# A hybrid encoder trunk on one core: the front re-cut into steps of two chunks, low parts on VectorE, kept parts in long rows

## The chip, the cores and the metric

The kernel runs on one core of one Trainium2 chip. The time is that of one execution on the device, in microseconds (us); lower is better. The engines are PE (TensorE: matrix products, with PEld as its weight loads), DVE (VectorE), ACT (ScalarE), POOL (GpSimd) and SP (SyncE, which here issues most transfers). Each engine takes its instructions strictly in program order and waits at the first one whose inputs are not there. Before the change: 1161.26 us, the median of 3 runs (1159.34 to 1162.54).

## The reference, cut to what matters

Two sequences of 512 rows (prompt and sample, 1024 wide) go through one layer with the same weights.

```
mod = silu(c) @ w_ada + b_ada                       # 1024 -> 6*1024
sh1, sc1, g1, sh2, sc2, g2 = split(mod, 6)
h = rms_norm(x, norm1_g) * (1 + sc1) + sh1
proj = h @ w_in                                     # 1024 -> 2816 columns
q_a, k_a, v_a, q_r, k_r, v_r, g_r = split(proj)     # the first 768 columns: q_a (512), k_a, v_a (128 each)
o_a = windowed_attention(q_a, k_a, v_a, sink)       # distance bias, |t-s| <= 128
o_r = bidirectional_retention(q_r, k_r, v_r, g_r, decay_fwd, decay_bwd)
x = x + g1 * (concat(o_a, o_r) @ w_out)
x = x + g2 * (relu(rms_norm(x, norm2_g)*(1+sc2)+sh2 @ w_mlp1)^2 @ w_mlp2)
y = rms_norm(x, final_g)
```

Products run in near fp32 precision: each fp32 operand is split into a high part (a cast) and a low part (operand minus high part), and a product is three matmuls, high by high, low by high and high by low.

## The kernel before, in words

The 1024-wide contraction is cut into eight chunks of 128, kc = 0 to 7. What this text calls the front runs from the start to the end of the first 768 projected columns of the prompt. It has to do three things that hang on one another, chunk by chunk.

*Modulation sums.* Only the shift and scale columns of w_ada are needed first. For chunks 0 and 1 there is one sum each (`one`); from chunk 2 on a pair of chunks has a scale sum (`pair(kc, 1)`, tiles named ..._1) and a shift sum (`pair(kc, 0)`, tiles ..._0). A pair's sum, in `ada_sums` (L206 to L239), is a generator in three steps: 16 small matmuls into `pm` (L216; 8 with high weights `wh_ada`, 8 with low weights `wl_ada`, the first 8 on one half of the rows, kh = 0, the last 8 on the other, kh = 1) and a copy by ACT of the sum to `mr` (L221); two transposes by PE into `pmt` (L229); and four small DVE operations that leave the shift or scale columns `mod_s`, `mod_a` (L232, L234, L202, L204). A weight tile's high part is a cast by ACT (`high_pair`, L97); its low part (`low_pair`, L1001) is a subtraction by DVE for kh = 0 and by POOL for kh = 1.

*Modulated chunks.* `prepare(kc)` calls `modulated` (L323): DVE forms `hm` = x transposed times scale plus shift (L326), ACT casts the high part `h` (L327), DVE subtracts for the low part (L328).

*Products.* `products(kc, c0, c1)` multiplies chunk kc by columns c0 to c1 of six column groups (L128 to L130, three matmuls each, into six open accumulators `first`). Its weights come from `split_wi(kc)`: the high part `wih` by DVE (ACT for chunk 0), the low part `wil` by POOL for all but one chunk. After the sixth column group, ACT issues two transfers that keep the previous chunk's `wih` and `wil` in `kept_first` (L1047), so that the sample sequence can read them back (`kept_unit`, L119) instead of splitting them again. There `kept_first` is laid out by column group: a partition's write is six pieces of 512 B, a partition's read one row of 4 KB.

Two side tasks run in between: the table of distance biases (`masked_distance` on DVE, L503, and eight ACT operations `bias_t`, L514, taken one at a time by `next(tables)`) and the retention decays (`log_decays`, L521).

The order on each engine is the order in which the code is written: everything from `start` to `pin(start)` is left as it stands, and a scheduler places only later work. So what stands ahead of what is set by the loop at L1104 to L1183.

Of the kernel before, what the change touches and what calls it, by code (L numbers as in the profile page):

```python
# [15 lines left out]
P = 128  # L16
# [14 lines left out]
def trunk_kernel(ctx, tc, x0, x1, c0, c1, w_ada, b_ada, norm1_g, w_in, attn_sink, decay_f, decay_b,  # L31
# [38 lines left out]
    def f(ap):  # L70
        return ap.bitcast(F32)
# [82 lines left out]
    dec = const.tile([P, 2, RH], F32, name="dec")  # L154
    nc.gpsimd.dma_start(dec[:, 0, :], decay_f.broadcast_to([P, RH]))
    nc.gpsimd.dma_start(dec[:, 1, :], decay_b.broadcast_to([P, RH]))
    sink = const.tile([P, AH], F32, name="sink")
    nc.gpsimd.dma_start(sink, attn_sink.broadcast_to([P, AH]))

# [343 lines left out]
    def masked_distance():  # L503
        nc.vector.tensor_scalar(sink8, sink, 8.0, None, ALU.mult)
# [132 lines left out]
    def proj_unit(hT, col, name, done):  # L637
        key = f"in{col}"

        def load():  # L640
            if hT is hT_of[1]:
                return kept_unit(key, name, P)
            return split_unit(cols_unit(w_in, 0, KC, col, P), name, nc.vector)
# [44 lines left out]
    def ret_v_units(hT, b):  # L688
# [3 lines left out]
        def unit(kq):  # L692
            key = f"rv{kq}"

            def load():
                if b == 1:
                    return kept_unit(key, f"rv{b}_{kq}", 512)
                return split_unit(cols_unit(w_in, kq * 2, 2, 1792, 512), f"rv{b}_{kq}", nc.vector)

# [36 lines left out]
    def out_units(b, late=None):  # L736
# [10 lines left out]
        def unit(hf, kq):  # L747
# [224 lines left out]

    xt0 += [load_x_tile(0, t) for t in range(2, NT)]
    wi, pairs = {}, {}
# [31 lines left out]

    def low_one(kc, kh, engine):
        t, w = ones[kc][kh]
        engine.tensor_sub(w[1], t, f(w[0]))
        ones[kc][kh] = [x.rearrange("p (c k n) -> p c k n", c=2, n=P) for x in w]  # L1010
# [6 lines left out]

    def split_wi(kc, engine=nc.vector, low=nc.gpsimd):
        w = [r4(f"wi{s}_{kc}").rearrange("p a n -> p (a n)")[:, :768] for s in "hl"]
        if engine is nc.scalar:  # L1020
            nc.scalar.copy(w[0], wi[kc][:, :768])
        else:
            nc.vector.tensor_copy(w[0], wi[kc][:, :768])
        low.tensor_sub(w[1], wi[kc][:, :768], f(w[0]))
        wi[kc] = w

    def take_xT(kc, pt):
        if kc % 2 == 0:
            pair = r4(f"xT_{kc}", F32)
            xT.extend([pair[:, 0, :], pair[:, 1, :]])  # L1030
        if kc % 2 == 0:
            nc.scalar.copy(xT[kc], pt)
        else:
            nc.vector.tensor_copy(xT[kc], pt)
# [4 lines left out]
    def products(kc, c0, c1):  # L1039
# [29 lines left out]
    cond = conditioning()  # L1069
    r0 = x_rstd(0, 0, xt0[0])  # L1070
    r1 = x_rstd(0, 1, xt0[1])
    x_scale(xt0[0], r0)
    next(cond)
    x_columns(0)
    next(cond)
    x_scale(xt0[1], r1)
    x_columns(1)
    r2 = x_rstd(0, 2, xt0[2])
    next(cond)
    r3 = x_rstd(0, 3, xt0[3])  # L1080
    x_scale(xt0[2], r2)
# [8 lines left out]
    split_wi(0, nc.scalar)  # L1090
    low_one(0, 1, nc.vector)
    for kc in range(4):
        take_xT(kc, banks[kc])
# [12 lines left out]
    first = attn_units(hT[0], 0)
# [3 lines left out]
    next(one1)  # L1110
    products(0, 1, 2)
# [8 lines left out]
    split_wi(2)  # L1120
    load_pair(4)
    load_wi(4)
    load_wi(5)
    g = pair(2, 1)
    next(g)
    products(1, 0, 1)
    next(g)
    high_pair(4, 1)
    g = pair(2, 0)
    next(g)  # L1130
    products(1, 1, 2)
    next(g)
    next(tables)
    prepare(2)
    low_pair(4, 1, 0, nc.vector)
    low_pair(4, 1, 1, nc.gpsimd)
    split_wi(3)
    prepare(3)
    products(1, 2, 6)
    logs = log_decays()  # L1140
    for kc in range(4, KC, 2):
        high_pair(kc, 0)
        low_pair(kc, 0, 0, nc.vector)
        if kc > 4:
            next(logs)
        low_pair(kc, 0, 1, nc.gpsimd)
        products(kc - 2, 0, 3)
        g = pair(kc, 1)
        next(g)
        products(kc - 2, 3, 5)  # L1150
        next(g)
        next(tables)
        split_wi(kc)
        if kc > 4:
            next(logs)
        products(kc - 2, 5, 6)
        g = pair(kc, 0)
        next(g)
        if kc + 2 < KC:
# [8 lines left out]
        next(logs)
        if kc + 2 < KC:
            low_pair(kc + 2, 1, 0, nc.vector)  # L1170
            low_pair(kc + 2, 1, 1, nc.gpsimd)
        split_wi(kc + 1, low=nc.gpsimd if kc == 4 else nc.vector)
        next(logs)
        prepare(kc + 1)
        next(logs)
        next(tables)
        products(kc - 1, 1, 6)
    next(tables)
    pin(start)
# [298 lines left out]
```

## Time and profile before

| | before |
|---|---|
| median of 3 runs | 1161.26 us |
| the profiled execution: its time, and its span | 1161.89 us, 1160.1 us |
| PE busy in the span | 1109.4 us (96%) |
| DVE, ACT, POOL busy | 933.4, 494.0, 69.0 us |
| PE's first matmul, first product, end of the front | 10.43, 23.27, 82.32 us |
| PE's granted clock, mean | 0.992 |

A share of busy time is an average; it is the idle time of PE, and what ended each piece of it, that tells what a stage waits for. In a row such as `65.20 0.28 PE L229 ... [2.13 <-ACT mr L221]` the first number is when the instruction starts, the second how long it takes, and the bracket how long the engine sat idle just before it and whose result ended that. "PEclk" is the clock granted to TensorE: 1.00 is the higher of its two levels (2.4 GHz), 0.50 the lower (1.2 GHz). POOL's 13 long operations of the front (six `wl_ada`, seven `wil`) all lie before 71 us.

### The profile page before, as it was taken

The numbers are of one execution on the slowest core, as the hardware profiler recorded it, in microseconds if no ns is written. First come the engines' busy times: TensorE is split into PE (matmuls) and PEld (weight loads), VectorE is DVE, ScalarE is ACT, GpSimd is POOL, SyncE is SP. The second block draws the span as 40 slices with busy tenths as digits, with TensorE's granted clock in tenths as the row PEclk, the third lists the DMA queues.
The fourth block names the chain that finished last, engine by engine and source line by source line (L and its number), as shares of the span: only waits on it lengthen the run. The fifth ranks groups of instructions, "written<-read, shape, count | busy, mean of one in ns | idle before, by whom it ended". The sixth has DMA issues, their size and how long they took to land.

```text
span 1160.1 us, 14470 instructions
## 1 busy us (share of the span) xinstructions
PE 1109.4 (96%) x5167; PEld 903.8 (78%) x5167; DVE 933.4 (80%) x1550; ACT 494.0 (43%) x846; POOL 69.0 (6%) x79
## 2 busy tenths in 40 slices
PE   5899999999999999999999999999999999999975
PEld 3578787777888788888788888888778888888854
DVE  5888988978888697689998778866696866968896
ACT  4456765435563234346333333332455333432341
POOL 3620001000000000000000000000000000000012
PEclk9999999999999999999999999999999999999988
DMA  9796677655455489941654455443866364464413
GB/s 289 238 283 211 214 230 272 218 193 190 155 167 199 156 303 333 343 148 46 214 204 155 164 165 189 155 163 103 287 230 237 106 195 137 144 200 139 184 37 145
DMA packets 124112, 224.37 MB, mean 193 GB/s; under 512 B 8500, under 2 KB 59780, under 8 KB 124040
## 3 DMA queue, kind: packets, MB, share of 16 engines
q1 hardware_dynamic: 111144, 217.14, 55.8%
q10 hardware_dynamic: 12544, 6.29, 1.9%
q8 instruction: 40, 0.66, 0.3%
q0 software_dynamic: 352, 0.03, 0.1%
q14 instruction: 32, 0.26, 0.1%
HBM read 152.36 MB, written 71.06 MB: 193 GB/s over the span
## 4 chain that ended last, share of the span: by engine, by line
PE 75%; DVE 11%; DMA 5%; issue 3%; ACT 3%; POOL 2%; SPq 0%; ACTq 0%; DVEq 0%; POOLq 0%
PE px_None L936 12%; PE x L1310 12%; PE py_None L936 9%; PE y L1310 9%; PE po L129 2%; PE po L130 2%; PE po L128 2%; DMA raw_ada_g<-in_w_ada_dram 2%; PE po L429 1%; PE ppt L422 1%; PE psc L396 1%; PE pj_rq L129 1%; PE pj_rq L128 1%; PE pj_rv L128 1%; PE pj_rv L130 1%
## 5 line engine op out<-in xcount | busy, mean ns | idle before, releaser
L841 ACT CAST uc_0h<-ur 128x1024 fp32r<-128x1024 f32 x28 | 29.4, 1050 | 67.9 <-PE x L1310 38.1
L1310 PE MATMUL x<-wc_0l,uc_0h 128*128 128x512 f32 x128 | 50.7, 396 | 5.4 <-DVE wc_0l L842 5.4
L1310 PE MATMUL x<-wc_0h,uc_0h 128*128 128x512 f32 x128 | 50.5, 396 | 3.9 <-DVE acc L1356 3.2
L128 PE MATMUL po<-wh_wo,ms 128*128 128x512 f32 x128 | 50.5, 397 | 1.9 <-ACT ms L761 1.9
L1310 PE MATMUL x<-wc_1h,uc_1h 128*128 128x512 f32 x128 | 50.3, 394 | 1.0 <-ACT wc_1h L841 1.0
L1310 PE MATMUL x<-wc_1l,uc_1h 128*128 128x512 f32 x128 | 50.2, 392 | 0.5 <-DVE wc_1l L842 0.5
L1310 PE MATMUL x<-wc_0h,uc_0l 128*128 128x512 f32 x128 | 50.3, 393 | 0.0
L1310 PE MATMUL x<-wc_1h,uc_1l 128*128 128x512 f32 x128 | 50.1, 391 | 0.0
L129 PE MATMUL po<-wl_wo,ms 128*128 128x512 f32 x128 | 49.8, 391 | 0.3 <-DVE wl_wo L103 0.3
L842 DVE TENSOR_TENSOR uc_0l<-ur,uc_0h 128x1024 fp32r<-128x1024 f32 x28 | 34.2, 1222 | 19.6 <-ACT uc_0h L841 15.9
L130 PE MATMUL po<-wh_wo,ms 128*128 128x512 f32 x128 | 49.6, 390 | 0.0
L255 DVE SCALAR_TENSOR_TENSOR adacc_c<-raw_ada_c,cact,adacc_c 128x512 f32<-128x512 f32 x56 | 39.8, 748 | 6.7 <-DMA raw_ada_c<-in_w_ada_dram 5.7
L841 ACT CAST wc_s4h<-raw_w 128x1024 fp32r<-128x1024 f32 x16 | 16.8, 1053 | 62.8 <-PE px_None L936 46.1
L406 ACT ACTIVATE st<-st,negm 128x256 f32<-128x256 f32 (+1 forms) x64 | 35.2, 556 | 18.8 <-DVE negm L401 18.8
L841 ACT CAST wc_0h<-w 128x1024 fp32r<-128x1024 f32 x24 | 25.2, 1049 | 42.4 <-DVE w L1289 16.3
L255 DVE SCALAR_TENSOR_TENSOR adacc_g<-raw_ada_g,cact,adacc_g 128x512 f32<-128x512 f32 x56 | 40.3, 747 | 2.1 <-DMA raw_ada_g<-in_w_ada_dram 1.8
L842 DVE TENSOR_TENSOR wc_0l<-w,wc_0h 128x1024 fp32r<-128x1024 f32 x24 | 29.3, 1221 | 13.5 <-ACT wc_0h L841 13.4
L936 PE MATMUL py_None<-hch,wc_a 128*128 128x512 f32 x120 | 39.7, 390 | 0.1
L936 PE MATMUL px_None<-hch,wc_a 128*128 128x512 f32 x120 | 39.6, 391 | 0.0
L936 PE MATMUL px_None<-hch,wc_s 128*128 128x512 f32 x120 | 39.4, 389 | 0.0
L1310 PE MATMUL y<-wc_1l,uc_1h 128*128 128x512 f32 x96 | 37.5, 391 | 0.6 <-DVE wc_1l L842 0.6
L1310 PE MATMUL y<-wc_0h,uc_0h 128*128 128x512 f32 x96 | 37.6, 392 | 0.0
(397 smaller groups left out, 3484.8 us busy)
## 6 DMA issues: line engine op xcount, KB each, us to landing
ur<-spill SPq DMA_DIRECT2D x56, 512.0 KB, 4.3
raw_w<-in_w_mlp_dram SPq DMA_DIRECT2D x32, 512.0 KB, 3.8
spill<-s SPq DMA_DIRECT2D x64, 256.0 KB, 3.7
w<-in_w_mlp_dram SPq DMA_DIRECT2D x32, 512.0 KB, 5.4
spill<-u SPq DMA_DIRECT2D x48, 256.0 KB, 2.3
raw_ada_g<-in_w_ada_dram SPq DMA_DIRECT2D x16, 512.0 KB, 4.3
raw_ada_c<-in_w_ada_dram SPq DMA_DIRECT2D x16, 512.0 KB, 4.0
raw_ada<-in_w_ada_dram SPq DMA_DIRECT2D x12, 512.0 KB, 8.8
```

Source lines behind the costliest of these rows:

```text
L128: nc.tensor.matmul(ps, lhs[0], rhs[0], start=start, stop=False)
L129: nc.tensor.matmul(ps, lhs[0], rhs[1], start=False, stop=False)
L130: nc.tensor.matmul(ps, lhs[1], rhs[0], start=False, stop=stop)
L255: nc.vector.scalar_tensor_tensor(acc[b], src, cb, acc[b], ALU.mult, ALU.add)
L396: nc.tensor.matmul(psc[:, :w], qs[hh][:, isl], k_[:, s, j0 * P:j1 * P], start=(s == 0), stop=(s == 1))
L406: nc.scalar.activation(st[hh][:, :w], st[hh][:, :w], AF.Exp, bias=negm[:, hh:hh + 1], scale=0.125, accum_out=den[:, hh:hh + 1])
L422: nc.tensor.transpose(pt[:, hh * P:(hh + 1) * P], st[hh][:, jj * P:(jj + 1) * P], ident)
L429: nc.tensor.matmul(po, va[:, j0 + jj, g].rearrange("p s e -> p (s e)"), pts[jj][:, s, :], start=(jj == 0 and s == 0), stop=(jj == nj - 1 a ...
L841: nc.scalar.copy(hi, src)
L842: nc.vector.tensor_sub(lo, src, f(hi))
L936: self.last = nc.tensor.matmul(bank[:, cs], x[:, k, :], y, start=first and k == 0 and i == 0, stop=last and k == 3 and i == 2, skip_group_ ...
L1310: nc.tensor.matmul(out, u[x][:, i % 2, ts_], w[y][:, i % 2, :], start=first and i == 0 and k == 0, stop=end and i == GP - 1 and k == 2, sk ...
```

## The change

The diff, without its renamed arguments and with the start of the front cut:

```
-                nc.scalar.dma_start(kept_first[:, :, s, k*P:(k+1)*P], f(wi[k][s]).rearrange(...))
-    kept_first = tc.dram_tile((P, 6, 2, 1024), F32, name="kept_first")
+                nc.scalar.dma_start(kept_first[:, s, k, :], f(wi[k][s]))
+    kept_first = tc.dram_tile((P, 2, KC, 768), F32, name="kept_first")

 def modulated(which, b, kc, src):
+    if which == b == kc == 0:                # chunk 0: two ACT activations straight from xT
+        for d in (dst[:, 0, :], t):
+            nc.scalar.activation(d, src, AF.Identity, bias=mod_s..., scale=mod_a...)
+        nc.vector.tensor_sub(dst[:, 1, :], t, f(dst[:, 0, :]))
+        return dst

-def low_pair(kc, s, kh, engine):             # low_one likewise
-    engine.tensor_sub(w[1], t, f(w[0]))
+def low_pair(kc, s, kh):
+    nc.vector.tensor_sub(w[1], t, f(w[0]))

-def split_wi(kc, engine=nc.vector, low=nc.gpsimd):    # high part: DVE (ACT for chunk 0), low: POOL
+def split_wi(kc):
+    nc.scalar.copy(w[0], wi[kc][:, :768])
+    nc.vector.tensor_sub(w[1], wi[kc][:, :768], f(w[0]))

     prepare(1)
+    low_pair(2, 1, 1)
     high_pair(2, 0)
-    low_pair(2, 0, 0, nc.vector)
-    low_pair(2, 0, 1, nc.gpsimd)
-    products(0, 2, 6)                        # and the hand-written steps for chunks 1 to 3, and the old loop
...
+    low_pair(2, 0, 0)
+    low_pair(2, 0, 1)
+    head_loads()                             # decays and sinks, on POOL's queue; before, at the start
+    tables, logs = None, log_decays()
+    for kc in range(2, KC, 2):
+        sums_a, sums_b = pair(kc, 1), pair(kc, 0)
+        more = kc + 2 < KC
+        next(sums_a)
+        products(kc - 2, 3 if kc == 2 else 0, 4 if kc == 2 else 3)
+        if more:                             # the loads of the next pair and its two chunks
+            load_pair(kc + 2); load_wi(kc + 2); load_wi(kc + 3)
+        next(sums_a)
+        split_wi(kc)
+        next(sums_b)
+        products(kc - 2, 4 if kc == 2 else 3, 6)
+        split_wi(kc + 1)
+        if more:
+            high_pair(kc + 2, 1); low_pair(kc + 2, 1, 0)
+        if kc > 2:
+            next(logs); next(logs)
+        next(sums_b)
+        prepare(kc)
+        if more:
+            low_pair(kc + 2, 1, 1)
+        prepare(kc + 1)
+        products(kc - 1, 0, 3)
+        if more:
+            high_pair(kc + 2, 0); low_pair(kc + 2, 0, 0); low_pair(kc + 2, 0, 1)
+        if tables is None:
+            tables = bias_tables(masked_distance())
+        for _ in range(3):
+            next(tables, None)
+        next(logs, None)
+        if kc == 2:
+            next(logs)
+        products(kc - 1, 3, 6)
     pin(start)
```

At the start of the front, the transposes of the first two x tiles now stand ahead of that of `ps_rows`, x tile 3 is loaded after the first sum's weights, and chunk 0's transposed x is copied by DVE instead of ACT. `kept_unit` reads the new layout: six weight tiles' two parts each, in pieces of 512 B.

Three places in the order matter for what follows. The first is ACT's program between the second chunk of a pair being modulated (`h_0_3`) and the copy of the next pair's shift sum (`mr_0`). Before:

```order
L327 CAST h_0_3_455<-hm_0_3_456 128x512
L1047 DMA kept_first<-wih_242 768x1x128
L1047 DMA kept_first<-wil_243 768x1x128
L97 CAST wh_ada_4_0_0_474<-raw_ada_4_0_0_367 128x1024
L97 CAST wh_ada_4_0_1_477<-raw_ada_4_0_1_369 128x1024
L221 COPY mr_1_508<-pm_1_491 4x256
L514 ACTIVATE bias_t<-di 128x384
L1047 DMA kept_first<-wih_288 768x1x128
L1047 DMA kept_first<-wil_289 768x1x128
L221 COPY mr_0_552<-pm_0_535 4x256
```

After the change:

```order
L335 CAST h_0_3_443<-hm_0_3_444 128x512
L97 CAST wh_ada_4_0_0_457<-raw_ada_4_0_0_371 128x1024
L97 CAST wh_ada_4_0_1_460<-raw_ada_4_0_1_373 128x1024
L521 ACTIVATE bias_t<-di 128x384 x3
L534 ACTIVATE lg_z<-lg_ax 128x8
L1052 DMA kept_first<-wih_250 128x768
L1052 DMA kept_first<-wil_251 128x768
L224 COPY mr_1_508<-pm_1_491 4x256
L1028 CAST wih_540<-raw_wi_375 128x768
L224 COPY mr_0_561<-pm_0_544 4x256
```

The copy `mr_1` of the scale sum of chunks 4 and 5 stood behind two casts; now it stands behind the two casts, three bias operations, `lg_z` and two transfers' issues, and the bias operations read `di`.

The second is DVE's program from `di`, the distance table, to the low part of the weights for the first pair sum. Before, where `wl_ada_2_1_1` is not on DVE but the third of POOL's long operations:

```order
L507 SCALAR_TENSOR_TENSOR di<-dl 128x384
L508 TENSOR_SCALAR di<-di 128x384
L509 TENSOR_TENSOR di<-di 128x384
L1023 CAST wih_288<-raw_wi_140 128x768
L1001 TENSOR_TENSOR wl_ada_2_1_0_293<-raw_ada_2_1_0_142,wh_ada_2_1_0_292 128x1024
L204 TENSOR_SCALAR mod_s_105<-pmt_316,cols 128x2
L202 TENSOR_SCALAR mod_a_103<-pmt_316,onep,cols 128x2
L1034 COPY xT_326<-px_7_328 128x512
L326 TENSOR_SCALAR hm_0_1_335<-xT_247,mod_a_103,mod_s_105 128x512
L328 TENSOR_TENSOR h_0_1_334<-hm_0_1_335,h_0_1_334 128x512
L1001 TENSOR_TENSOR wl_ada_2_0_0_340<-raw_ada_2_0_0_146,wh_ada_2_0_0_339 128x1024
```

After the change, the same place (chunk 1's modulation and the pair's low parts):

```order
L1029 TENSOR_TENSOR wil_281<-raw_wi_137,wih_280 128x768
L1009 TENSOR_TENSOR wl_ada_2_1_0_285<-raw_ada_2_1_0_139,wh_ada_2_1_0_284 128x1024
L207 TENSOR_SCALAR mod_s_102<-pmt_310,cols 128x2
L205 TENSOR_SCALAR mod_a_100<-pmt_310,onep,cols 128x2
L1039 COPY xT_320<-px_7_322 128x512
L334 TENSOR_SCALAR hm_0_1_329<-xT_254,mod_a_100,mod_s_102 128x512
L336 TENSOR_TENSOR h_0_1_328<-hm_0_1_329,h_0_1_328 128x512
L1009 TENSOR_TENSOR wl_ada_2_1_1_288<-raw_ada_2_1_1_141,wh_ada_2_1_1_287 128x1024
L1009 TENSOR_TENSOR wl_ada_2_0_0_335<-raw_ada_2_0_0_143,wh_ada_2_0_0_334 128x1024
L1009 TENSOR_TENSOR wl_ada_2_0_1_338<-raw_ada_2_0_1_145,wh_ada_2_0_1_337 128x1024
```

The low part for kh = 1 of the first pair sum, `wl_ada_2_1_1`, now comes on DVE behind chunk 1's copy, `hm` and low part.

The third is DVE's program at the end of the first new step, where the table is now built:

```order
L336 TENSOR_TENSOR h_0_2_437<-hm_0_2_438,h_0_2_437 128x512
L1009 TENSOR_TENSOR wl_ada_4_1_1_425<-raw_ada_4_1_1_369,wh_ada_4_1_1_424 128x1024
L334 TENSOR_SCALAR hm_0_3_444<-xT_267,mod_a_100,mod_s_102 128x512
L336 TENSOR_TENSOR h_0_3_443<-hm_0_3_444,h_0_3_443 128x512
L1009 TENSOR_TENSOR wl_ada_4_0_0_458<-raw_ada_4_0_0_371,wh_ada_4_0_0_457 128x1024
L1009 TENSOR_TENSOR wl_ada_4_0_1_461<-raw_ada_4_0_1_373,wh_ada_4_0_1_460 128x1024
L514 SCALAR_TENSOR_TENSOR di<-dl 128x384
L515 TENSOR_SCALAR di<-di 128x384
L516 TENSOR_TENSOR di<-di 128x384
L529 TENSOR_SCALAR sink_104<-sink 128x8
L532 SCALAR_TENSOR_TENSOR lg_ax<-dec 128x8
```

`di` has moved from ahead of `wl_ada_2_1_0` to behind the four low parts of the next pair and both chunks of this one.

## Rows read from the trace of the kernel before

**Rows 1.** Windows: us, busy us of each engine, PEclk, DMA share, GB/s.

```profile
67.00:68.00 1.00, 1.00 (x6) 0.64 (x5) 0.90 (x5) 0.00 (x0) 0.42 (x1) 0.50 1.15 348
120.00:280.00 160.00, 156.76 (x753) 125.60 (x751) 140.47 (x306) 86.42 (x176) 9.90 (x12) 1.00 0.66 218
1118.00:1119.00 1.00, 1.00 (x3) 0.74 (x3) 1.00 (x3) 0.00 (x0) 0.00 (x0) 0.50 0.00 0
```

**Rows 2.** PE's waits from 0 to 82 us: total, times, longest.

```profile
PE pmt L229 <- ACT mr L221: 2.5, 2, 2.1
PE pm L216 <- DVE wl_ada L1001: 1.8, 1, 1.8
PE first L129 <- DVE h L328: 1.3, 3, 0.8
...
PE first L128 <- ACT h L327: 0.8, 1, 0.8
PE pm L216 <- POOL wl_ada L1001: 0.4, 1, 0.4
```

**Rows 3.** Timeline of PE: a pair sum, then the first matmuls of a product.

```profile
35.85 0.28 PE L216 MATMUL pm<-wl_ada,c 128*4 128x256 f32 x1 [1.77 <-DVE wl_ada L1001]
...
37.60 0.40 PE L128 MATMUL first<-h,wih 128*128 128x512 f32 x1
37.83 0.39 PE L129 MATMUL first<-h,wih 128*128 128x512 f32 x1
```

**Rows 4.** Timeline of PE: the last pair sum of the front.

```profile
65.20 0.28 PE L229 MATMUL pmt<-ident,mr 4*128 4x4 f32 x2 [2.13 <-ACT mr L221]
...
66.36 0.42 PE L216 MATMUL pm<-wl_ada,c 128*4 128x256 f32 x1
...
69.35 0.42 PE L216 MATMUL pm<-wl_ada,c 128*4 128x256 f32 x1
```

**Rows 5.** Timeline of PE: the longest wait late in the kernel.

```profile
1115.88 0.79 PE L1310 MATMUL x<-wc_0l,uc_0h 128*128 128x512 f32 x1 [5.42 <-DVE wc_0l L842]
1116.47 0.63 PE L1310 MATMUL x<-wc_0h,uc_0l 128*128 128x512 f32 x1
...
1120.74 0.52 PE L1310 MATMUL y<-wc_0l,uc_0h 128*128 128x512 f32 x1
```

**Rows 6.** Timeline of DVE in the front.

```profile
24.53 0.55 DVE L507 SCALAR_TENSOR_TENSOR di<-dl 128x384 f32<-128x384 f32 x1
...
27.91 0.68 DVE L1034 COPY xT<-px 128x512 f32<-128x512 f32 x1
...
36.57 4.06 DVE L202 TENSOR_SCALAR mod_a<-ms,onep,cols 128x2 f32<-128x2 f32 x2
...
42.42 0.69 DVE L328 TENSOR_TENSOR h<-hm,h 128x512 fp32r<-128x512 f32 x1 [0.68 <-ACT h L327]
43.03 1.22 DVE L1001 TENSOR_TENSOR wl_ada<-raw_ada,wh_ada 128x1024 fp32r<-128x1024 f32 x1
...
44.64 0.54 DVE L326 TENSOR_SCALAR hm<-xT,mod_a,mod_s 128x512 f32<-128x512 f32 x1
```

**Rows 7.** DVE by shape, 20 to 82 us: busy us, mean ns, idle before.

```profile
L1024 DVE TENSOR_TENSOR wil<-raw_wi,wih 128x768 fp32r<-128x768 f32 x1 | 1.0, 959 | 0.0
```

**Rows 8.** ACT by shape, 10 to 82 us.

```profile
L97 ACT CAST wh_ada<-raw_ada 128x1024 fp32r<-128x1024 f32 x14 | 14.1, 1044 | 2.1 <-DMA raw_ada<-in_w_ada_dram 1.1 <-issue 0.9
L327 ACT CAST h<-hm 128x512 fp32r<-128x512 f32 x8 | 5.0, 620 | 18.1 <-DVE hm L326 18.0
L514 ACT ACTIVATE bias_t<-di 128x384 bf16<-128x384 f32 x8 | 4.2, 520 | 1.0 <-issue 1.0
L221 ACT COPY mr<-pm 4x256 f32<-4x256 f32 x7 | 2.5, 361 | 11.8 <-PE pm L216 11.8
```

**Rows 9.** Timeline of ACT: one issue of a kept part.

```profile
61.62 0.52 ACTq L1047 DMA_DIRECT2D kept_first<-wih  x1
```

**Rows 10.** The tile wh_q, read back for the sample: durations, first and last start.

```profile
L119 SPq DMA_DIRECT2D wh_q<-kept_first x4: 319/319/412, 220.6 to 236.2; - x4
```

More of the change, by code (lines that the diff above doesn't have):

```diff
@@ L154, in trunk_kernel, with head_loads @@
     dec = const.tile([P, 2, RH], F32, name="dec")
-    nc.gpsimd.dma_start(dec[:, 0, :], decay_f.broadcast_to([P, RH]))
-    nc.gpsimd.dma_start(dec[:, 1, :], decay_b.broadcast_to([P, RH]))
     sink = const.tile([P, AH], F32, name="sink")
-    nc.gpsimd.dma_start(sink, attn_sink.broadcast_to([P, AH]))
+    def head_loads():
+        nc.gpsimd.dma_start(dec[:, 0, :], decay_f.broadcast_to([P, RH]))
+        nc.gpsimd.dma_start(dec[:, 1, :], decay_b.broadcast_to([P, RH]))
+        nc.gpsimd.dma_start(sink, attn_sink.broadcast_to([P, AH]))
     cols = const.tile([P, 80], F32, name="cols")
@@ L325, in modulated @@
         t = f2(f"hm_{which}_{b}_{kc}")
+        if which == b == kc == 0:
+            for d in (dst[:, 0, :], t):
+                nc.scalar.activation(d, src, AF.Identity, bias=mod_s[0][:, kc, 0:1], scale=mod_a[0][:, kc, 0:1])
+            nc.vector.tensor_sub(dst[:, 1, :], t, f(dst[:, 0, :]))
+            return dst
         nc.vector.tensor_scalar(t, src, mod_a[which][:, kc, b:b + 1], mod_s[which][:, kc, b:b + 1], ALU.mult, ALU.add)
@@ L642, in load @@
                 return kept_unit(key, name, P)
-            return split_unit(cols_unit(w_in, 0, KC, col, P), name, nc.vector)
+            return split_unit(cols_unit(w_in, 0, KC, col, P), name)
         def use(w):
@@ L697, in load @@
                     return kept_unit(key, f"rv{b}_{kq}", 512)
-                return split_unit(cols_unit(w_in, kq * 2, 2, 1792, 512), f"rv{b}_{kq}", nc.vector)
+                return split_unit(cols_unit(w_in, kq * 2, 2, 1792, 512), f"rv{b}_{kq}")
             def use(w):
@@ L970, in store @@
                 nc.sync.dma_start(spill[g][p, :, i, :], t)
-    xt0 += [load_x_tile(0, t) for t in range(2, NT)]
+    xt0.append(load_x_tile(0, 2))
     wi, pairs = {}, {}
@@ L1005, in high_one, with low_one @@
         ones[kc][kh] = ones[kc][kh], split_high(ones[kc][kh], f"ada1_{kc}_{kh}", spare_ws)
-    def low_one(kc, kh, engine):
+    def low_one(kc, kh):
         t, w = ones[kc][kh]
-        engine.tensor_sub(w[1], t, f(w[0]))
+        nc.vector.tensor_sub(w[1], t, f(w[0]))
         ones[kc][kh] = [x.rearrange("p (c k n) -> p c k n", c=2, n=P) for x in w]
@@ L1016, in pair @@
         return ada_sums(f"{kc}_{s}", [pairs[kc, s, kh] for kh in range(2)], lambda c, m: first_mod(s == 1, kc + c, m))
-    def split_wi(kc, engine=nc.vector, low=nc.gpsimd):
+    def split_wi(kc):
         w = [r4(f"wi{s}_{kc}").rearrange("p a n -> p (a n)")[:, :768] for s in "hl"]
[L1020 to L1024, printed above, removed]
+        nc.scalar.copy(w[0], wi[kc][:, :768])
+        nc.vector.tensor_sub(w[1], wi[kc][:, :768], f(w[0]))
         wi[kc] = w
@@ L1030, in take_xT @@
             xT.extend([pair[:, 0, :], pair[:, 1, :]])
-        if kc % 2 == 0:
+        if kc % 2 == 0 and kc > 0:
             nc.scalar.copy(xT[kc], pt)
@@ L1057, in trunk_kernel @@
         ones.append(load_one(kc))
+        if kc == 0:
+            xt0.append(load_x_tile(0, 3))
         load_wi(kc)
@@ L1069, in trunk_kernel @@
     cond = conditioning()
[L1070 to L1081, printed above, removed]
+    for t in range(2):
+        x_scale(xt0[t], x_rstd(0, t, xt0[t]))
+        x_columns(t)
+    for _ in range(3):
+        next(cond)
+    x_scale(xt0[2], x_rstd(0, 2, xt0[2]))
     x_columns(2)
-    x_scale(xt0[3], r3)
-    x_columns(3)
     high_one(0, 0)
-    low_one(0, 0, nc.vector)
+    low_one(0, 0)
     one0, one1 = one(0, stops=(3,), paired=True), one(1, stops=(1, 5))
@@ L1089, in trunk_kernel @@
     high_one(0, 1)
[L1090 to L1093, printed above, removed]
+    low_one(0, 1)
+    r3 = x_rstd(0, 3, xt0[3])
     next(one0)
-    next(one1)
+    x_scale(xt0[3], r3)
+    x_columns(3)
+    split_wi(0)
+    take_xT(0, banks[0])
     next(one0)
     prepare(0)
+    for kc in range(1, 4):
+        take_xT(kc, banks[kc])
+    next(one1)
     next(one1)
@@ L1110, in trunk_kernel @@
     next(one1)
-    products(0, 1, 2)
+    products(0, 1, 3)
     next(one1)
@@ L1115, in trunk_kernel @@
     prepare(1)
+    low_pair(2, 1, 1)
     high_pair(2, 0)
-    low_pair(2, 0, 0, nc.vector)
-    low_pair(2, 0, 1, nc.gpsimd)
-    products(0, 2, 6)
[L1120 to L1159, printed above, removed]
+    low_pair(2, 0, 0)
[8 more added lines that the diff above has]
+        if more:
             load_pair(kc + 2)
@@ L1162, in trunk_kernel @@
             load_wi(kc + 3)
-            high_pair(kc + 2, 1)
-        products(kc - 1, 0, 1)
-        next(g)
-        next(tables)
-        prepare(kc)
[L1168 to L1173, printed above, removed]
-        prepare(kc + 1)
[L1175 to L1178, printed above, removed]
+        next(sums_a)
[4 more added lines that the diff above has]
+        if more:
+            high_pair(kc + 2, 1)
+            low_pair(kc + 2, 1, 0)
+        if kc > 2:
+            next(logs)
+            next(logs)
+        next(sums_b)
+        prepare(kc)
+        if more:
+            low_pair(kc + 2, 1, 1)
+        prepare(kc + 1)
+        products(kc - 1, 0, 3)
+        if more:
+            high_pair(kc + 2, 0)
+            low_pair(kc + 2, 0, 0)
+            low_pair(kc + 2, 0, 1)
+        if tables is None:
+            tables = bias_tables(masked_distance())
+        for _ in range(3):
+            next(tables, None)
+        next(logs, None)
+        if kc == 2:
+            next(logs)
+        products(kc - 1, 3, 6)
     pin(start)
```

19 lines of the change are left out of this document (8 added, 11 removed).

## The prediction

> **What bounds the kernel now.** First the windows: from 120 to 280 us PE is busy 156.76 of 160 us [rows 1]. PE sets the time, and a change gains only what PE spends waiting or at the lower clock. Then PE's waits over the front [rows 2]: 2.5 us for ACT's copy `mr`, 1.8 for a low part by DVE and 0.4 for one by POOL, 1.3 and 0.8 for the two parts of `h`: 6.8 us in all, between the first product and the front's end. The timeline around the two long ones shows what waiting does to the clock. After the 1.77-us wait a pair sum still runs 15 matmuls in 1.75 us, 0.117 each, and a product's matmuls follow at 0.23 [rows 3]. After the 2.13-us wait, the last pair sum runs at 0.213 each (14 in 2.99 us) [rows 4], in a window whose PEclk is 0.50, the lower level [rows 1]. Those 3.2 us at half clock lost 1.6. The other long wait followed by work, 5.42 us, did the same: PEclk 0.50 and matmuls 0.43 apart from 1116.47 to 1120.74, 4.3 us that lost 2.1 [rows 1, 5]. So each of these two waits cost itself and about 1.6 to 2.1 us more.
>
> **The change part by part.**
>
> *What goes.* Every wait inside the front is re-dealt, so its old ones go: 6.8 us less 0.2 of the first chunk's, which I count below, is 6.5 (rounded), and the lost clock of 1.6. In sum −8.1.
>
> *DVE and POOL.* POOL loses six low parts of 1024 and seven of 768. DVE takes them at 1.22 [rows 6] and 0.96 [rows 7], 14.0 us, and hands seven casts of 768 to ACT. In return DVE's stretched operations should shrink: two 128x2 operations took 4.06 us at 36.57, while POOL ran [rows 6]. DVE's total falls or stays; that says nothing yet on PE, since the new order decides who waits.
>
> *Start.* Chunk 0 no longer passes through `hm` on DVE (0.54), but its transposed x is now copied behind more DVE work (0.68) [rows 6]; I set these against one another. The low part now waits for a second ACT pass of 0.62 [rows 8] and then DVE's 0.69 [rows 6]; the first product's own matmul covers about 0.4 of this, which leaves a wait near 0.9 where there was 0.2. I take +0.7, with bounds of −0.5 and +1.3.
>
> *Wait A, first pair sum.* PE issues this sum directly behind the last transposes, and its second half needs `wl_ada_2_1_1`. On DVE that stands behind chunk 1's x copy (0.68), `hm` (0.54), ACT's cast (0.62), the low part (0.69), then itself (1.22): 3.75 us after those transposes [rows 6, 8]. PE has eight matmuls of 0.117 meanwhile, 0.94 [rows 3]. Wait A is 2.8 (bounds 2.0 and 3.2).
>
> *Wait B, shift and scale of chunks 4 and 5.* I follow both engines from the end of the second pair sum. The chain that ends in `mr_1`: ACT's `mr` 0.36, a cast of 768 (at most a 1024's 1.04; I take 0.75), a cast of 1024 at 1.04 [rows 8]; DVE's low part 1.22 [rows 6], four small operations, about 0.65 (estimated); then for chunk 2 `hm` 0.54, cast 0.62, low part 0.69, a pair's low part 1.22; for chunk 3 0.54, 0.62, 0.69; two more low parts at 1.22; the three operations of `di`, about 1.4 (the first is 0.55) [rows 6]; ACT's three bias operations at 0.52, `lg_z`, two issues of 0.4 to 0.5 [rows 9], and `mr` 0.36 [rows 8]. That is 15.9 with operations overlapped where one follows another on an engine. PE has in that time: the last two column groups of chunk 0 (two products of three matmuls at 0.23, 1.4), the transposes (0.3), the six of chunk 1 (4.1), a pair sum (16 at 0.117, 1.9) in which it waits 0.5 for a low part, and three products of chunk 2 (2.1) [rows 3], with gaps 10.5. The difference, 5.4, is wait B. In the kernel before, `mr` stood ahead of the bias operations and `di` was begun at 24.5 us, long before its first use [rows 6]. Bounds 4.0 and 6.2; I take 5.2, since a sum of durations overstates a chain a little.
>
> *Wait C, chunks 6 and 7.* The same, but `di` exists by then, and a cast of the next weights (1.04) [rows 8] is scheduled between `h_4` and `h_5`. The chain from the end of the pair sum is about 14.5 by the same rows, PE's work 11.9. Wait C is 2.6 (bounds 0.5 and 3.0); I take 2.3.
>
> *Small ones.* PE waits near 0.5 for the transposes of chunk 1's sum and 0.5 and 0.3 for the kh = 1 low parts of two pair sums: +1.3.
>
> *The clock.* A and B are longer than the wait that lowered it: +1.6 each by [rows 4]. C lies so near to the two bounds that I take half, +0.8. Together +4.0 (bounds 0 and 5.3).
>
> *Long rows.* Sixteen ACT issues, 0.52 each at best before [rows 9], get shorter, but only where ACT stands on PE's path; wait B has that. The reads now come in 512-B pieces. `wh_q`'s four are issued from 220.6 to 236.2 [rows 10], well ahead of use, and PE's stalls there are part of only 3.2 us in 160 [rows 1]. I take +0.3 (bounds 0 and 2).
>
> *Later.* A front that ends later finds later weights landed: of the 3.2 us that PE idles from 120 to 280 [rows 1] I give back 1.2 (bounds 0 and 3).
>
> Sum: +0.7 − 8.1 + 2.8 + 5.2 + 2.3 + 1.3 + 4.0 + 0.3 − 1.2 = +7.3. The profiled execution took 1161.89, span 1160.1 and 1.8 around it; the median is 0.6 lower. So 1169.2 on that execution's scale and 1168.6 on the median's. I forecast 1168.
>
> **The rivals.** A measurement here can tell 0.3%, 3.5 us: faster is below 1157.8, slower above 1164.7.
>
> *Faster: POOL's hold on DVE decides.* If DVE, freed of POOL, runs ahead of PE through the whole front, the re-dealt waits are short. Two operations that touch two columns took 4.06 us there [rows 6], nearly all of it to be had back, and POOL has 13 long operations, so there is room. The Trainium skill, "SBUF — State Buffer", section "SBUF: two separate sides", has the port pair that DVE and GpSimd share as an exclusive lock held for a whole instruction; by that, every stretch goes with POOL's long operations, which the 4.06 us bear out as far as one row can. Against it: my chain in B uses durations without a stretch already, and is still 5 us too long. If A, B and C fall under 1 us each, the clock stays up and the sum is +0.7 − 8.1 + 3 + 1.3 − 1 = −4.1: 1157. It decides once B's chain comes down from 15.9 to about 11. Chance 0.10.
>
> *No change: the waits come, the clock stays.* With A, B and C at their lower bounds (6.5) and at most one lowered clock (1.6): 0.7 − 8.1 + 6.5 + 1.3 + 1.6 + 0.3 − 1.2 = +1.1, 1162. For it: only two waits in the trace show the lowered clock, and the work around them differs. Chance 0.20.
>
> *Slower still: ACT falls further behind.* The copy for the last shift sum stands behind a cast of the next weights; if its transfer is late, PE waits up to 3 us more. With that, B at its upper bound and B's clock at the 2.1 of [rows 5]: +3 + 1.0 + 0.5 is 1173. Chance 0.20.
>
> **How the numbers follow.** The forecast, 1168, has 0.50, its own range 1164 to 1171. Faster gets 0.10. From the forecast's lower edge (0.05) and the no-change case (0.16 of its 0.20, with 0.04 above the bound) come 0.21 for the same; the rest, 0.69, is slower. The range 1159 to 1173.5 leaves out most of the faster case and the tail above.
>
> **What would show it right or wrong.** PE's waits after: a wait of 2 to 3 us for `wl_ada` of the first pair sum, near 30 us; one of 4 to 6 for `mr` near 48; one near 66; PEclk 0.50 behind the first two; POOL empty of long operations and no 128x2 operation of DVE above 0.4 us; the first `pj_rv` product near 89 instead of 82.3. If no wait for `mr` exceeds 2 us, step B is wrong and the kernel is faster. If the waits are there and PEclk stays 1.00, the clock's term goes. If PE's stalls from 200 to 280 us grow, it is the 512-B reads.

## The result, and the profile after

The changed kernel takes 1164.64 us (median of 19 runs, 1163.38 to 1168.84) against 1161.40 (19 runs) for the kernel before: a ratio of 1.0029, 95% interval 1.0020 to 1.0037. The forecast was 1168, slower; the time lies inside the range, and the change is half as large as forecast. By the prediction's own bounds (the same up to 1164.7, slower above) it stands on the line between the two. The profiled execution has a span of 1162.5 us, 2.4 more than before.

PE's waits in the front, first by the view that groups them (engine, line, releaser: total, times, longest):

```profile
PE pmt L232 <- ACT mr L224: 6.6, 2, 4.6
PE pm L219 <- DVE wl_ada L1009: 3.6, 2, 2.7
...
PE first L130 <- DVE h L332: 0.9, 1, 0.9
PE first L129 <- ACT h L335: 0.6, 1, 0.6
```

Against before [rows 2], the waits for `h` and for POOL are gone or smaller, and those for `mr` (6.6 us instead of 2.5) and for low parts by DVE (3.6 instead of 1.8) are larger. The timeline of PE gives each its place:

```profile
7.29 3.02 PE L1073 MATMUL px<-ident,x 128*128 128x128 f32 x12 [7.29 <-DVE rv_x L307]
10.11 0.34 PE L173 MATMUL ps_rows<-ident,rows 80*128 80x80 f32 x1
...
23.37 0.50 PE L130 MATMUL first<-h,wih 128*128 128x512 f32 x1 [0.93 <-DVE h L332]
...
31.63 0.38 PE L219 MATMUL pm<-wl_ada,c 128*4 128x256 f32 x1 [2.69 <-DVE wl_ada L1009]
...
51.49 0.28 PE L232 MATMUL pmt<-ident,mr 4*128 4x4 f32 x2 [4.58 <-ACT mr L224]
...
68.83 0.28 PE L232 MATMUL pmt<-ident,mr 4*128 4x4 f32 x2 [1.99 <-ACT mr L224]
```

The first two rows are the new start: twelve transposes run from 7.29 us, in time in which PE before stood still for the transfer of the rows:

```profile
10.43 0.37 PE L170 MATMUL ps_rows<-ident,rows 80*128 80x80 f32 x1 [10.43 <-DMA rows<-in_b_ada_dram]
```

Then come the three large waits that the prediction called A, B and C: 2.69 us for the low part of the first pair sum, 4.58 and 1.99 for `mr`. The first `pj_rv` product starts at 86.58 us instead of 82.32.

The windows (columns as in [rows 1]) tell what the waits did to the clock, and what came back:

```profile
32.00:33.00 1.00, 1.00 (x7) 0.62 (x5) 1.00 (x2) 0.00 (x0) 0.00 (x0) 0.50 0.94 337
52.00:53.00 1.00, 1.00 (x7) 0.55 (x5) 0.96 (x4) 0.17 (x1) 0.00 (x0) 0.50 0.71 277
69.00:70.00 1.00, 1.00 (x11) 0.72 (x11) 0.89 (x7) 0.51 (x1) 0.00 (x0) 1.00 0.86 197
120.00:280.00 160.00, 158.19 (x763) 127.02 (x762) 141.69 (x312) 87.53 (x179) 9.57 (x12) 1.00 0.68 220
```

PEclk is 0.50 behind A and behind B, as behind the 2.13-us wait of before [rows 1, 4], and 1.00 behind C. From 120 to 280 us PE idles 1.8 us where it idled 3.2 [rows 1]. ACT's timeline ahead of B shows the chain's end:

```profile
49.73 0.52 ACT L521 ACTIVATE bias_t<-di 128x384 bf16<-128x384 f32 x1 [2.93 <-DVE di L516]
49.89 0.34 ACTq L1052 DMA_DIRECT2D kept_first<-wih  x1
50.16 0.51 ACT L521 ACTIVATE bias_t<-di 128x384 bf16<-128x384 f32 x1
50.27 0.45 ACTq L1052 DMA_DIRECT2D kept_first<-wil  x1
50.58 0.51 ACT L521 ACTIVATE bias_t<-di 128x384 bf16<-128x384 f32 x1
50.99 0.19 ACT L534 ACTIVATE lg_z<-lg_ax 128x8 f32<-128x8 f32 x1
51.09 0.34 ACT L224 COPY mr<-pm 4x256 f32<-4x256 f32 x1
```

ACT had sat 2.93 us for `di`; then the three bias operations and `lg_z` pass, and `mr` follows at 51.09. The two issues of kept parts (ACTq) run beside them and hold nothing: that of `wih` starts at 49.89, ahead of the second bias operation at 50.16, though it stands behind all three and `lg_z` in the program. So the strict order of which the text speaks at its start holds here among an engine's computing instructions, and not between these and the issues of transfers. POOL does nothing between PE's first product and its first `pj_rv` product, and the operations on two columns (`mod_a`) that took up to 2.44 us before take at most 0.29, as the prediction wanted to see.

### The profile page after: what moved, and what is told of

Read it like the earlier page. It is cut to its first block, busy times and chain, and to the rows that moved or that the text cites. A ratio compares the mean times of both kernels' runs of the same rounds, so it can differ in the third digit from the quotient of the medians.

```text
span 1162.5 us, 14461 instructions
## 1 busy us (share of the span) xinstructions
PE 1108.9 (95%) x5167; PEld 903.3 (78%) x5167; DVE 928.3 (80%) x1556; ACT 498.8 (43%) x853; POOL 38.8 (3%) x66
## 4 chain that ended last, share of the span: by engine, by line
PE 77%; DVE 10%; DMA 5%; ACT 4%; issue 2%; POOL 1%; ACTq 0%; DVEq 0%; POOLq 0%; SPq 0%
PE px_None L944 13%; PE x L1291 12%; PE py_None L944 9%; PE y L1291 9%; PE po L130 2%; PE po L131 2%; PE po L129 2%; PE po L437 1%; PE psc L404 1%; PE ppt L430 1%; PE pj_rv L129 1%; PE pj_rv L131 1%; PE pj_rv L130 1%; PE pj_rq L131 1%; PE pj_rq L129 1%
## 5 line engine op out<-in xcount | busy, mean ns | idle before, releaser
L1291 PE MATMUL y<-wc_0l,uc_0h 128*128 128x512 f32 x96 | 37.7, 392 | 0.0
```

What stands on the lines that cost most here:

```text
L1291: nc.tensor.matmul(out, u[x][:, i % 2, ts_], w[y][:, i % 2, :], start=first and i == 0 and k == 0, stop=end and i == GP - 1 and k == 2, sk ...
```

## The experiments

Each run was timed beside the kernel before on the same chip; ratios are to that kernel. The changed kernel itself stands at 1.0029, and runs are compared by these ratios.

**The table earlier.** In the changed kernel:

```
-        if tables is None: tables = bias_tables(masked_distance())      # at the end of the step
-        for _ in range(3): next(tables, None)
         next(sums_a)
+        if tables is None: tables = bias_tables(masked_distance())
         split_wi(kc)
+        for _ in range(3): next(tables, None)
         next(sums_b)
```

> The changed kernel, with the distance table built and its bias operations issued behind the copy of the first pair sum instead of behind the low parts at the step's end. Theory (order: what stands ahead of the copy mr sets PE's wait): the chain that ends in mr loses three table operations (about 1.4 us) and three bias operations (about 1.3), so PE's 4.6-us wait falls to 1.6 to 2.2, the 2.0-us one of the next step to under 1, PEclk stays 1.00 behind them, the first pj_rv product comes near 82 instead of 86.6, and with some of that returned later the time is 1160 to 1162, about 3.5 below the changed kernel. Rival (load: DVE and ACT simply have too much to do): the waits move but do not shrink, same time as the changed kernel within 1 us. Rival (repaid: what the front gains is lost again at later waits for weights): front 82, but time within 1.5 us of the changed kernel.

Measured: ratio 1.0017 (1.0006 to 1.0027). That is 1.4 us better than the changed kernel, not 3.5, and the two intervals overlap. The one execution with a trace took 3938.59 us and is not in the ratio, so the kernel was run once more for its trace:

> The same kernel as in the first run of the early table, for its profile. Theory (order, as there): PE's 4.6-us wait for mr is 1.6 to 2.5. Rival: the wait is there, but another has taken what it gave (one named by the trace), which would explain why the time fell by only 0.7 us.

Measured: ratio 1.0012 (1.0001 to 1.0022), 2.0 us better than the changed kernel, first `pj_rv` product at 86.7 us, no earlier than there. PE's timeline of that run, its waits:

```profile
31.60 0.37 PE L219 MATMUL pm<-wl_ada,c 128*4 128x256 f32 x1 [2.72 <-DVE wl_ada L1009]
...
38.88 0.28 PE L232 MATMUL pmt<-ident,mr 4*128 4x4 f32 x2 [0.74 <-ACT mr L224]
...
51.40 0.28 PE L232 MATMUL pmt<-ident,mr 4*128 4x4 f32 x2 [2.88 <-ACT mr L224]
...
68.29 0.28 PE L232 MATMUL pmt<-ident,mr 4*128 4x4 f32 x2 [1.70 <-ACT mr L224]
```

and ACT ahead of the wait at 38.88 and of that at 51.40:

```profile
37.23 1.35 ACT L521 ACTIVATE bias_t<-di 128x384 bf16<-128x384 f32 x3 [2.79 <-DVE di L516]
38.48 0.34 ACT L224 COPY mr<-pm 4x256 f32<-4x256 f32 x1
...
50.05 0.21 ACT L534 ACTIVATE lg_z<-lg_ax 128x8 f32<-128x8 f32 x1 [1.63 <-DVE lg_ax L532]
...
50.98 0.36 ACT L224 COPY mr<-pm 4x256 f32<-4x256 f32 x1 [0.72 <-ACT lg_z L534]
```

B fell from 4.58 to 2.88 and C from 1.99 to 1.70, 2.0 together. But ACT now sits 2.79 us for `di` ahead of the shift sum's `mr`, which PE awaits for 0.74 us; `lg_z`, still in the old place, holds the next `mr` to 50.98; and this time PEclk is 0.50 from 69 to 72 us, behind the wait of 1.70, where the changed kernel's wait of 1.99 left it at 1.00. The theory holds for the wait and fails for the time: a side task moved out of one chain was put into the next.

**One low part earlier.** In the changed kernel:

```
     low_pair(2, 1, 0)
+    low_pair(2, 1, 1)
...
     prepare(1)
-    low_pair(2, 1, 1)
```

> The changed kernel, with one line moved: the kh = 1 low part of the first pair sum stands on DVE ahead of chunk 1's modulation instead of behind it. Theory (order): PE's 2.7-us wait near 31 us falls to 1 to 2, the half-clock stretch of 3 us behind it goes (1.5 us), front ends 2 to 3 us earlier (84), time 1162 to 1163. Rival (load): chunk 1 is late in its place and PE waits as long there; 1164.6.

Measured: ratio 1.0029 (1.0015 to 1.0043), as the changed kernel; first `pj_rv` product at 88.4. Wait A is gone, and a wait for `mr` stands one product (three matmuls) further on. PE, then ACT ahead of it:

```profile
33.22 0.34 PE L232 MATMUL pmt<-ident,mr 4*128 4x4 f32 x2 [2.10 <-ACT mr L224]
...
33.88 0.41 PE L219 MATMUL pm<-wh_ada,c 128*4 128x256 f32 x1
34.09 0.41 PE L219 MATMUL pm<-wl_ada,c 128*4 128x256 f32 x1
```

```profile
30.39 0.62 ACT L335 CAST h<-hm 128x512 fp32r<-128x512 f32 x1 [1.60 <-DVE hm L334]
30.92 1.99 ACT L97 CAST wh_ada<-raw_ada 128x1024 fp32r<-128x1024 f32 x2
32.81 0.36 ACT L224 COPY mr<-pm 4x256 f32<-4x256 f32 x1
```

`mr` was ready to be copied at about 30.3 us, when the sum ended; ACT was on chunk 1's cast, which hung on DVE and now came later, and then on two casts of 1024. The low clock (0.21 a matmul) now falls on a whole pair sum. C grew as well, from 1.99 to 2.89 us, and lowered the clock, which it did not in the changed kernel. The rival (PE waits as long there) came out.

**Low parts back on POOL, in the new order.**

```
-        nc.vector.tensor_sub(w[1], t, f(w[0]))                          # low_pair
+        (nc.gpsimd if kh else nc.vector).tensor_sub(w[1], t, f(w[0]))
-    nc.vector.tensor_sub(w[1], wi[kc][:, :768], f(w[0]))                # split_wi
+    (nc.gpsimd if kc < 7 else nc.vector).tensor_sub(w[1], ...)
```

> The changed kernel in its new order, but with the kh = 1 low parts and seven of the eight weights' low parts back on POOL, as before. Theory (the order loses, freeing DVE from POOL gains): DVE's small operations stretch again beside POOL, a 128x2 pair takes 2 to 4 us, the wait for mr grows from 4.6 to 6 or 7, front ends 1 to 3 us later (88 to 90), time 1166 to 1168. Rival (load: DVE is what is late, POOL was of help): DVE has 14 us less, waits shrink, time 1161 or less.

Measured: 1169.63 us, ratio 1.0076 (1.0056 to 1.0096), first `pj_rv` product at 91.3: 4.7 us later than with DVE. The theory holds, and more strongly than expected. DVE and POOL in the first step:

```profile
33.57 7.59 DVE L205 TENSOR_SCALAR mod_a<-ms,onep,cols 128x2 f32<-128x2 f32 x1
41.08 1.21 DVE L1009 TENSOR_TENSOR wl_ada<-raw_ada,wh_ada 128x1024 fp32r<-128x1024 f32 x1
```

```profile
34.57 0.55 POOL L161 DMA_DIRECT2D sink<-in_attn_sink_dram  x1
35.12 3.68 POOL L1029 TENSOR_TENSOR wil<-raw_wi,wih 128x768 fp32r<-128x768 f32 x2
38.73 2.39 POOL L1009 TENSOR_TENSOR wl_ada<-raw_ada,wh_ada 128x1024 fp32r<-128x1024 f32 x1
```

An operation of two columns on DVE lasts 7.59 us, until POOL's third long operation ends at 41.1; it had started before the first of them. The 4.06 us of [rows 6] are two such operations, of 1.71 and 2.44 us, which ended with POOL's subtractions at 38.2 and 40.6. The Trainium skill, "SBUF — State Buffer", section "SBUF: two separate sides", calls the shared port pair an exclusive lock held by one engine for a whole instruction; that DVE's operation ends with POOL's agrees with it, though here one outlasts three of POOL's. POOL's own pace is part of the loss too: a low part of 1024 takes it 2.39 us and DVE 1.21, and PE waits 1.4 us in all for those of POOL. The run does not part the two.

**The old order with all low parts on DVE and the first weights' casts on ACT.**

```
-        low_pair(kc, 0, 1, nc.gpsimd)                                   # and the five like it
+        low_pair(kc, 0, 1, nc.vector)
-    def split_wi(kc, engine=nc.vector, low=nc.gpsimd):
+    def split_wi(kc, engine=nc.scalar, low=nc.vector):
```

> The kernel before, in its old order, with only the engines changed: all low parts on DVE and all casts of the first weights on ACT. Theory (freeing DVE from POOL is the gain of the change, its order the loss): DVE loses its stretches (4.06 us for one pair of small operations among them), waits for wl_ada and h shrink, the front ends 3 to 4 us earlier than before (78 to 79.5), time 1156 to 1159. Rival (load): DVE takes 14 us more and hands over 4, PE waits longer for mr, time 1162 or more. Rival (repaid later): front 79, time within 1.5 us of before.

Measured: ratio 0.9995 (0.9983 to 1.0007), first `pj_rv` product at 82.7, in an execution in which PE's first matmul came 0.4 us later than before: no gain. Waits for `wl_ada` and `h` shrank to 0.8 and 0.2 us, but `mr` costs 5.1 in three waits (0.94, 1.69, 2.44), and PEclk falls to 0.50 behind the second and third. ACT ahead of these two:

```profile
45.09 0.58 ACTq L1047 DMA_DIRECT2D kept_first<-wih  x1
45.70 0.67 ACTq L1047 DMA_DIRECT2D kept_first<-wil  x1
46.41 1.05 ACT L97 CAST wh_ada<-raw_ada 128x1024 fp32r<-128x1024 f32 x1 [0.71 <-issue]
...
63.23 1.04 ACT L97 CAST wh_ada<-raw_ada 128x1024 fp32r<-128x1024 f32 x1 [0.89 <-issue]
63.41 2.17 ACTq L1047 DMA_DIRECT2D kept_first<-wih  x1
```

ACT's cast at 46.41 sat 0.71 us, that at 63.23 0.89 us, for "issue": the queue was still issuing the kept parts' 512-B pieces, 0.5 to 2.2 us each. This suggested that with DVE freed the issues on ACT are what is late next; the next runs test it.

**The kept parts in short pieces again, in the new order.** The layout lines of the diff taken back:

```
-    kept_first = tc.dram_tile((P, 2, KC, 768), F32, name="kept_first")
+    kept_first = tc.dram_tile((P, 6, 2, 1024), F32, name="kept_first")
```

> The changed kernel with only the layout of the kept parts as before (writes in six 512-B pieces a partition, reads in 4-KB rows). Theory (issue: an issue of 512-B pieces holds ACT, as in the old order with low parts on DVE, where ACT sat 0.7 and 0.9 us behind issues ahead of mr): the 4.6-us and 2.0-us waits for mr grow by 0.5 to 1.5 each, the second one now lowers the clock, front ends 88 to 90, time 1166 to 1168. Rival (long rows do nothing, ACT only issues): waits as in the changed kernel within 0.3 us, time 1164.6. Rival (reads in 512-B pieces cost later): front as before, stalls of PE from 200 to 280 us smaller by 1 us or more, time 1163.

Measured: 1174.02 us, ratio 1.0087 (1.0067 to 1.0108), first `pj_rv` product at 92.0. Long rows are worth 0.6% in this order. The waits B (4.77) and C (1.90) are as in the changed kernel, though C now lowers the clock, as the theory had it. The larger loss is at the front's end:

```profile
75.28 0.83 ACT L1028 CAST wih<-raw_wi 128x768 fp32r<-128x768 f32 x1 [2.19 <-issue]
...
77.94 3.68 ACTq L1052 DMA_DIRECT2D kept_first<-wil  x1
81.67 0.62 ACT L335 CAST h<-hm 128x512 fp32r<-128x512 f32 x1 [5.55 <-issue]
```

```profile
82.34 2.08 PE L129 MATMUL first<-h,wih 128*128 128x512 f32 x4 [3.95 <-ACT h L335]
```

ACT sits 5.55 us ahead of that cast, most of it during an issue of 3.68 us, and PE waits 3.95 us for `h` where it waited 0.6 in the changed kernel. So issues do hold PE, but at another place than the theory named. The trace is of the fastest of four executions (1168.50 us; the others 1173.62 to 1175.29): what cost those 5 us more is not shown.

**The long rows alone, in the kernel before.** The same lines the other way, and nothing else:

```
-    kept_first = tc.dram_tile((P, 6, 2, 1024), F32, name="kept_first")
+    kept_first = tc.dram_tile((P, 2, KC, 768), F32, name="kept_first")
```

> The kernel before with only the kept parts in long rows. Theory (issue): ACT is free earlier ahead of the last mr, the 2.1-us wait falls to about 1.2 and the half-clock stretch behind it (1.6 us) goes, front ends near 80, time 1158.5 to 1160. Rival (nothing): 1161.4 within 1 us. Rival (reads cost later): PE's stalls from 200 to 280 us grow and the time is 1162 or more.

Measured: ratio 0.9992 (0.9979 to 1.0006), first `pj_rv` product at 81.4, 0.9 us earlier than before. The last wait for `mr` falls from 2.13 to 1.78 us and leaves the clock up, but the wait of 1.77 us at 36 us, unchanged in place and length, now lowers it (PEclk 0.50 from 36 to 39) where it did not before [rows 3]. In the time, the rival that nothing changes came out.

**Both together in the old order.** Low parts on DVE, long rows, and one cast moved:

```
-    split_wi(2)
...
     g = pair(2, 1)
     next(g)
+    split_wi(2)
     products(1, 0, 1)
```

> The kernel before in its old order, with low parts on DVE, first-weight casts on ACT, kept parts in long rows, and the cast of chunk 2's weights moved behind the first pair's mr. Theory (the change's order is its loss; freeing DVE and long rows are gains, which only show together since the issues of short pieces hold ACT where DVE is freed): waits for mr 0, 1.2 and 1.8 instead of 0.9, 1.7 and 2.4, front ends 78 to 80, time 1156 to 1158.5. Rival (load): waits for mr over 1.5 us each remain, front 82, time 1161. Rival (repaid later): front 79, time 1160 or more.

Measured: 1156.66 us, ratio 0.9945 (0.9933 to 0.9958): faster than both kernels: 6.0 us less than the one before, timed beside it, and, ratio to ratio, 0.8% less than the changed one, with the first `pj_rv` product at 77.5. PE's waits, and ACT at the place shown for the run without long rows:

```profile
35.02 0.28 PE L230 MATMUL pmt<-ident,mr 4*128 4x4 f32 x2 [0.21 <-ACT mr L222]
...
47.64 0.28 PE L230 MATMUL pmt<-ident,mr 4*128 4x4 f32 x2 [1.19 <-ACT mr L222]
...
61.94 0.28 PE L230 MATMUL pmt<-ident,mr 4*128 4x4 f32 x2 [1.48 <-ACT mr L222]
```

```profile
44.84 0.45 ACTq L1048 DMA_DIRECT2D kept_first<-wil  x1
45.33 1.05 ACT L97 CAST wh_ada<-raw_ada 128x1024 fp32r<-128x1024 f32 x1 [0.25 <-issue]
```

The hold for "issue" is 0.25 instead of 0.71 us, no wait for `mr` passes 1.5, and PEclk stays 1.00 behind all of them. The theory holds for the three edits together; the moved cast was not run apart.

**The start of the change, before the old steps.** The changed kernel, with everything from `split_wi(1)` to `pin(start)` replaced by the old sequence as in the last run, the distance table's place included:

> The changed kernel's start (transposes of the first two x tiles ahead of that of the rows, chunk 0 by two ACT passes, x tile 3 loaded later), engines and long rows, with the steps behind it in the old order and chunk 2's cast behind mr, as in the run before that was faster than both kernels. Theory (order: the start of the change is a gain, its steps the loss): second product at 23.4 as in the changed kernel instead of 25.6, later waits as in that run (1.2 and 1.5 for mr, clock up), front ends 75.5 to 77, time 1154 to 1156. Rival (engine load): the earlier start only lengthens the waits for mr to 2 us or more, time as that run, 1156.7, or more.

Measured: 1158.47 us, ratio 0.9956 (0.9939 to 0.9973), first `pj_rv` product at 78.0. The second product stands at 23.26 us, 2.3 earlier than in the last run (25.57), and that is given back: 0.53 and 0.70 us of new waits for `mr`, and a wait of 1.55 us that lowered the clock from 62 to 65 us. By the time the rival came out: this run and the last one can't be told apart.

```profile
PE pmt L232 <- ACT mr L224: 4.0, 4, 1.6
```

This run against the changed kernel is nearly the changed steps alone: 4.0 us of waits for `mr` against 6.6, none for low parts against 3.6, 78.0 against 86.6 us at the front's end, 0.7% in the time.

**Two casts earlier on ACT, kept parts from POOL's queue.**

```
     split_wi(3)
+    high_pair(4, 0)                              # likewise high_pair(kc + 2, 0) in the loop
     prepare(3)
...
-                    nc.scalar.dma_start(kept_first[:, s, k, :], f(wi[k][s]))
+                    nc.gpsimd.dma_start(kept_first[:, s, k, :], f(wi[k][s]))
```

> As the run beside it, with two more edits: the casts of the next shift sum's weights on ACT moved ahead of the second chunk's modulation, and the kept parts written from POOL's queue. Theory (what stands on ACT ahead of mr sets PE's wait): the waits for mr of 1.2 and 1.5 fall under 0.7 and no ACT time goes to issues; front 75 to 76, time 1153 to 1155.5. Rival (the buffers and loads behind those casts become late in turn): a wait for h of chunk 6 or 7 or for the next weights of 1 to 2 us appears, time as the run beside it or 1 us more.

Measured: 1153.19 us, ratio 0.9925 (0.9911 to 0.9939), first `pj_rv` product at 75.9, the best of all. Its waits:

```profile
PE pmt L232 <- ACT mr L224: 2.2, 3, 1.0
PE first L130 <- DVE h L332: 0.9, 1, 0.9
```

The two waits of 1.2 and 1.5 us for `mr` are gone, none is left above 1.0, and PEclk stays 1.00 from 20 us to the front's end. The two edits were not run apart.

## Why the prediction was right, and where its sizes were off

*The place and the cause of the waits* came out: A 2.8 forecast and 2.69 measured, B 5.2 and 4.58, C 2.3 and 1.99, each behind the named instruction. That the steps' order makes the loss is shown by the run with the old steps behind the same start (0.9956 against 1.0029): the change is a loss of 0.7% by its steps and a gain of 0.4% by the rest of it (with one cast moved). That taking the low parts from POOL is a gain in this order is shown by the run with POOL (1.0076).

*What each single edit would save* the prediction did not ask, and the runs say less than the waits do: taking A away moved the time by 0, and 1.7 us off B by 1.4 and 2.0 us in its two runs, since the next wait for ACT took most of A's, and the new wait of 0.74 with the clock behind C took about as much as B and C lost up to the front's end.

*Start: +0.7 forecast, −0.6 measured* (second product at 23.37 instead of 23.99). The step weighed only chunk 0's modulation: its wait came as forecast (0.93), but the transposes moved ahead of `ps_rows` filled time in which PE stood still for the rows' transfer, and the first sum began at 14.5 instead of 17.3 us. They were not in the sum. Part of these 2.8 us was lost again: the first sum now ran at PEclk 0.50 until 17.5 us, where it had 1.00 before. Against the same engines with the old start (second product at 25.48 and 25.57 in the two runs of the old order) the new start is worth about 2 us.

*The clock: +4.0 forecast.* A and B each left some 3 us at PEclk 0.50, 1.5 lost apiece; C's 0.8 did not come in that execution: +3.0. The runs show that this term was less certain than I made it (last section).

*The sum.* Between the first product and the first `pj_rv` product PE idles 11.9 us (64.64 less 52.78 busy) instead of 6.8, and is busy 0.5 longer, the lower clock included; the first product comes 1.3 earlier (21.94 against 23.27). That is +4.3 at the front's end, where the prediction's terms made +8.2. The terms as measured (start −0.6, what goes −8.1, A to C 9.3, two small waits 0.9 and 0.6, clock 3.0) make +5.1; the 0.8 between I can't place. Of the small waits, that of 0.6 for `h` was not named. In B, the chain lasted 14.7 us, from the pair sum's end near 36.7 to the end of `mr` at 51.4, instead of 15.9, and PE had 10.2 us of work. The 15.9 is what the listed durations add up to with nothing overlapped, against what the prediction says of it; the two issues in it (some 0.9) ran beside the bias operations and cost nothing, which is most of the overestimate.

*Later: −1.2 forecast.* From 120 to 280 us PE idles 1.4 less and from 400 to 520 another 0.5, so most of the way from +4.3 to the span's +2.4 is in those two stretches.

*Long rows: +0.3, hidden, forecast.* Here the reasoning failed, though the result did not show it. Short pieces in the new order cost 0.6%. As far as the trace shows it, this came by ACT held at the front's end, a place that the prediction did not look at. The reads in 512-B pieces cost nothing visible in the changed kernel (no stall for them in its trace); in the run with the new start one `wl_q` was awaited 1.3 us.

*The rival "faster"* named a gain that is there, but its condition, A to C under 1 us each, did not come: the new order outweighed it. In the old order the freed DVE and the long rows each show no gain alone (0.9995 and 0.9992), and 0.9945 together with one moved cast.

*The other two rivals* did not come either. For "no change" the waits had to be 6.5 us and lower the clock once; they were 9.3 and lowered it twice. For "slower still" the copy of the last shift sum had to be late; PE did not wait for it.

What stays open: why a wait of the same length lowers the clock in one execution and not in the next, and how much of the last run's gain is the casts' and how much the queue's, and what the moved cast has of the gain of 0.9945.

## What to carry to other kernels

Follow one chain through all its engines, instruction by instruction, before moving a side task: the copy that PE waits for was late because of what stood ahead of it on ACT, and ACT because of what stood ahead on DVE. A wait removed is worth only its distance to the next one, so move the work behind the copy rather than into the neighbouring chain, and count an issue of many small pieces as time of the engine that issues it.

## What the runs showed of the hardware that was not expected

The length of PE's wait did not tell whether the granted clock fell. Behind 1.55 us (new start, old steps), 1.69 (old order, low parts on DVE), 1.70 (table early), 1.90 (short rows) and 2.10 (low part earlier) PEclk went to 0.50 for some 3 us; behind 1.94 (before, at 405.6 us), 1.98 and 2.37 (low parts on POOL) and 1.99 (after) it stayed at 1.00. One and the same wait gave both: 1.77 us near 36 left it up in the kernel before and lowered it with long rows alone; A, 2.69 us near 31, lowered it in the changed kernel and left it at 1.00 with short rows. So a term for the clock is a spread, about 1.5 us a wait that may or may not come. It can be more: behind B in the run with the low part earlier (4.58 us) PE worked at 0.50 for some 5 us, from 52.0 to 57.1. An operation of two columns on DVE lasted 7.59 us beside POOL's long ones. And ACT's issue of a transfer began ahead of computing instructions that stand before it in ACT's program (49.89 against 50.16 us).
